# Modulated activations: who writes the rounded half of a high/low pair, and from where

## The chip, the cores and the metric

One core of a Trainium2 chip runs the whole program. The metric is device microseconds from launch to end, median of several executions; lower is better. Engine names in the profile: PE is TensorE, DVE is VectorE, ACT is ScalarE, POOL is GpSimd, SP is SyncE (it only issues transfers here).

## What is computed

Two small transformer blocks, one after the other, on 256 tokens of width 1024, all in float32. The change is in the second block, in the step that prepares the input of a matrix product: a norm, then a scale and a shift per feature (`modulate`). It occurs once for the pooled context, once for the context before the attention, and three times for the tokens.

```python
def rms_norm(x, g):
    y = x * lax.rsqrt(jnp.mean(x * x, axis=-1, keepdims=True) + EPS)
    return y * g

def modulate(h, shift, scale):
    return h * (1 + scale[:, None, :]) + shift[:, None, :]

# second_block, one layer
m_l = modulate(rms_norm(h_lat, norm_g[i, 1]), sh2, sc2)
h_lat = h_lat + g2[:, None, :] * sq_relu_mlp(m_l, mlp_w1[i], mlp_w2[i])
```

## The kernel before

Every product is made to float32 accuracy from three products of rounded halves: a matrix X is kept as a pair, X high (rounded to the type `F32R`) and X low (X minus its high half, in the same type), and `mm3` (lines 248 to 251) adds high x high, high x low and low x high in PSUM. Weights arrive by DMA as raw tiles of 128x1024; `split` makes their pair, with one activation on ScalarE (line 241) and two subtractions of 512 columns on VectorE (line 244), into a ring of seven slots. These "weight splits" run ahead of the products for the whole program.

An activation has 256 tokens, as two halves t of 128, and 1024 features, as 8 chunks k of 128 columns in the transposed layout. `mod_feed` (line 1102) handles one half t after the other, and in it four chunks at a time (n = 0, 1): VectorE scales the tokens by their reciprocal norm (line 1108, tile `mxn`), TensorE transposes four blocks into one PSUM bank of 512 columns (line 1111, tile `mtp`; two such banks take turns, and in the context's case they are shared with the products `cfo`), and then each block of 128 columns is multiplied by a column `g` and shifted by a column `b`, into the staging tile `m` (name `mmx`, two of them). `NACT` is 2: the first two of four blocks are done by ScalarE (line 1118), the others by VectorE (line 1120); in the call for layer 0 and the tokens all four are ScalarE's. Then `hilo_v` on VectorE makes the pair from `m`: a copy of 512 columns that rounds (line 259, a CAST in the profile), and a subtraction (line 260). With `mark` set, the last activation of half 0 becomes the mark `fed`: weight splits number 4 to 6 after it are told to wait for it on their engines.

`mod_xt` (line 1021) does the same for the pooled context, with 256 columns per chunk (both halves t) and two chunks per bank, so four banks; all scaling is ScalarE's (line 1038). Its staging tile shares a pool of three buffers with the two `mxn` tiles and others.

The order of the instructions on each engine is fixed when the program is built: a scheduler takes, for each engine, the ready instruction with the highest priority (by place in the program) by its own estimate of times. A buffer's next user waits until its last reader is done.

The places where these steps run, named here for later (start times in us of the profiled execution):

| place | what | lines | from, to |
|---|---|---|---|
| A | `mod_xt` in `ctx_pool`, beside the junction of `ple_block` | 1021 to 1040 | 1189, 1206 |
| B | `mod_feed` in `mlp0`, tokens, layer 0 | 1102 to 1124 | 1220, 1232 |
| C | `mod_feed` at the end of `mlp0`, context, layer 1; `cfo` products and `acc` products around it | 1102 to 1124, 1271 | 1552, 1574 |
| D | `mod_feed` in `attn_block` through `k_groups`, tokens; products `ckv` before, `lkv` behind | 1102 to 1124, 1348 | 1579, 1592 |
| E | `mod_feed` in `mlp1`, tokens, with `mark`; products `g` behind (24 per half) | 1102 to 1124, 1286 | 1708, 1730 |

Of the kernel before, what the change touches and what calls it, by code (L numbers as in the profile page):

```python
# [9 lines left out]
F32 = mybir.dt.float32  # L10
# [3 lines left out]
AF = mybir.ActivationFunctionType  # L14
ALU = mybir.AluOpType
# [8 lines left out]
NACT = 2  # L24
# [146 lines left out]
def tile_model(ctx: ExitStack, tc: tile.TileContext, A, out):  # L171
    nc = tc.nc
    V, S, G, T, Y = nc.vector, nc.scalar, nc.gpsimd, nc.tensor, nc.sync
# [24 lines left out]
    for t in range(2):  # L198
        for n in range(2):
            sl = slice(512 * n, 512 * n + 512)  # L200
# [57 lines left out]
    def hilo_v(hi, lo, src):  # L258
        V.tensor_copy(hi, src)
        V.tensor_tensor(lo, src, hi.bitcast(F32), op=ALU.subtract)  # L260

    def bank(r=None, name="bk"):
        r = r or M
        return r.bank.tile([128, 512], F32, name=name + r.tag, tag="bk" + r.tag)
# [22 lines left out]
    def rstd_of(src):  # L287
        return ms_r(ssq2(halves(src), 1.0 / 32), epst[:, 0:1])[1]
# [145 lines left out]
    def xk(xt, k, t):  # L434
        return xt[0][:, k, 128 * t:128 * t + 128], xt[1][:, k, 128 * t:128 * t + 128]
# [537 lines left out]
    gsc = cp.tile([128, 2, 2, 2, 8], F32, name="gsc")  # L973
# [47 lines left out]
    def mod_xt(src, l, v, j, sh, xt, al, r=None):  # L1021
        xn = []
        for t in range(2):
            rs = rstd_of(src[:, t])
            x = al([128, 1024], "mxn")
            V.tensor_scalar(x, src[:, t], rs, None, op0=ALU.mult)
            xn.append(x)
        for q in range(4):
            ps = bank(r, "mtp")
            for i in range(2):  # L1030
                for t in range(2):
                    T.transpose(ps[:, 256 * i + 128 * t:256 * i + 128 * t + 128],
                                xn[t][:, 256 * q + 128 * i:256 * q + 128 * i + 128], ident)
            m = al([128, 512], "mmx")
            for i in range(2):
                k = 2 * q + i
                sl = slice(256 * i, 256 * i + 256)
                S.activation(m[:, sl], ps[:, sl], AF.Identity, scale=gsc[:, l, v, j, k:k + 1], bias=sh[:, k:k + 1])
            hilo_v(xt[0][:, 2 * q:2 * q + 2].rearrange("p a c -> p (a c)"),
                 xt[1][:, 2 * q:2 * q + 2].rearrange("p a c -> p (a c)"), m)  # L1040

    def alloc_in(pool, bufs=2):
        def al(shape, name, dt=F32):
# [58 lines left out]
    def mod_feed(rr, l, v, j, sh, xt, al, src=None, r=None, mark=False):  # L1102
        src = h if src is None else src
        for t in range(2):
            rs = rr(t)
            for n in range(2):
                xn = al([128, 512], "mxn")
                V.tensor_scalar(xn, src[:, t, 512 * n:512 * n + 512], rs, None, op0=ALU.mult)
                ps = bank(r, "mtp")
                for i in range(4):  # L1110
                    T.transpose(ps[:, 128 * i:128 * i + 128], xn[:, 128 * i:128 * i + 128], ident)
                m = al([128, 512], "mmx")
                for i in range(4):
                    k = 4 * n + i
                    sl = slice(128 * i, 128 * i + 128)
                    g, b = gsc[:, l, v, j, k:k + 1], sh[:, k:k + 1]
                    if i < (4 if not l and not v else NACT):
                        sa = S.activation(m[:, sl], ps[:, sl], AF.Identity, scale=g, bias=b)
                    else:
                        V.tensor_scalar(m[:, sl], ps[:, sl], g, b, op0=ALU.mult, op1=ALU.add)  # L1120
                sl = (slice(None), slice(4 * n, 4 * n + 4), slice(128 * t, 128 * t + 128))
                hilo_v(xt[0][sl], xt[1][sl], m.rearrange("p (k c) -> p k c", k=4))
                if t == 0 and mark:
                    fed[:], cnt[:] = [sa.ins], [0]

# [7 lines left out]
    def ctx_pool(cx):  # L1133
        wk = cx.work
        al = u4(wk)
        hc = cx.sp.tile([128, 2, 1024], F32, name="hc", tag="hc")
        for t in range(2):
            Y.dma_start(hc[:, t], A["ctx"][128 * t:128 * t + 128])
        pool_pt(hc, hc, *prow(1, wk, "u4", 3), al, cx.xt, cx)
        hc = cx.sp.tile([128, 2, 1024], F32, name="hc", tag="hc")  # L1140
        for t in range(2):
            Y.dma_start(hc[:, t], A["ctx"][128 * t:128 * t + 128])
        gg = al([128, 1024], "crow")
        Y.dma_start(gg, rows[6].partition_broadcast(128))
        for n in range(2):
            w = split(cx, A["plw"], n)
            for t in range(2):
                ps = bank(cx, "cpm")
                for j in range(4):
                    g = 2 * n + j // 2  # L1150
                    sl = slice(256 * j, 256 * j + 256)
                    mm3(ps[:, 256 * (g % 2):256 * (g % 2) + 256], xk(cx.xt, 2 * g + j % 2, t), (w[0][:, sl], w[1][:, sl]),
                        j % 2 == 0, j % 2 == 1)
                y = al([128, 512], "cpy")
                V.tensor_tensor(y, ps, gg[:, 512 * n:512 * n + 512], op=ALU.mult)
                hs = hc[:, t, 512 * n:512 * n + 512]
                V.tensor_tensor(hs, hs, y, op=ALU.add)
        cx.hc = hc
        cx.xt = xt_tiles(8, cx.xp, "cxT")
        mod_xt(hc, 0, 1, 1, adacol[:, 0, 1, 24:32], cx.xt, al, cx)  # L1160
# [15 lines left out]
    def mlp0(rr, cx, pre):  # L1176
        with tc.tile_pool(name="lm0", bufs=1, reuse_waits="tile") as lm:
# [4 lines left out]
            xt = xt_tiles()  # L1182
            al = alloc_in(lm)
            mod_feed(rr, 0, 0, 1, adacol[:, 0, 0, 24:32], xt, al)

            def splits(w):
# [73 lines left out]
            def rstd(t):  # L1260
# [8 lines left out]
                return rstd_of(cx.hc[:, t])  # L1269

            mod_feed(rstd, 1, 1, 0, adacol[:, 1, 1, 0:8], cxt, al, cx.hc, cx)
            cx.xt = cxt
            for t in range(2):
# [7 lines left out]
    def mlp1(rr, cx):  # L1281
        with tc.tile_pool(name="lm1", bufs=1, reuse_waits="tile") as lm:
            g = gload(rows[8 + 3])
            xt = xt_tiles()
            al = alloc_in(lm)
            mod_feed(rr, 1, 0, 1, adacol[:, 1, 0, 24:32], xt, al, mark=True)

            def first():
# [345 lines left out]
```

## Time and profile before

| what | value |
|---|---|
| median of 3 executions | 1907.61 us (1907.52 to 1912.47) |
| the profiled execution | 1908.55 us |
| its span, first to last instruction | 1906.4 us |
| TensorE busy | 1838.0 us, 96% |
| VectorE busy | 1336.7 us, 70% |
| ScalarE busy | 923.3 us, 48% |
| GpSimd busy | 55.8 us, 3% |
| granted TensorE clock, mean | 0.991 of full speed |

Busy shares are means over the whole span; the stages of the change are five stretches of 10 to 22 us each, and a stage is read in the timeline of its own stretch: which engine stands still, and what ended its wait.

### The profile page before, as it was taken

The page shows a single profiled execution, that of the slowest core. Times are in us where ns is not written, and L with a number is a line of the kernel's source. Part 1 is how long each engine was busy: PE and PEld are TensorE (multiplying, and loading weights), DVE is VectorE, ACT ScalarE, POOL GpSimd, SP SyncE. Part 2 cuts the span into 40 slices and gives each one's busy share as a digit, 9 for nine tenths or more (in the row PEclk, how much of TensorE's full clock was granted, in tenths as well). Part 3 has the DMA queues.
Part 4 walks back from the last instruction along what each step waited for, and adds up shares of the span by engine and source line. Part 5 has one row for each costly group of instructions (what it writes and reads, how often), then busy time and mean ns, then how long its engine had stood idle before and what let it go on. Part 6 is the DMA issues. An engine that isn't in the chain of part 4 may idle for free.

```text
span 1906.4 us, 29714 instructions
## 1 busy us (share of the span) xinstructions
PE 1838.0 (96%) x11425; PEld 1617.3 (85%) x11425; DVE 1336.7 (70%) x2531; ACT 923.3 (48%) x1452; POOL 55.8 (3%) x96
## 2 busy tenths in 40 slices
PE   7999999999989999999999998899999999999998
PEld 6999777899969998888789897898999987667997
DVE  6997676899679986765587877854444468656555
ACT  6545656544474445444454455632322335544443
POOL 0000000000000000000000000000000002000000
PEclk9999999999999999999999999999999999999999
DMA  8887534788568876655488867433233224225662
GB/s 266 291 273 235 171 103 143 256 277 279 167 217 275 268 245 197 224 166 168 159 279 306 306 200 258 131 116 95 90 109 99 90 68 140 84 62 184 198 193 82
DMA packets 100950, 356.07 MB, mean 187 GB/s; under 512 B 12248, under 2 KB 13128, under 8 KB 100808
## 3 DMA queue, kind: packets, MB, share of 16 engines
q1 hardware_dynamic: 100088, 353.30, 57.0%
q8 instruction: 89, 1.46, 0.3%
q10 hardware_dynamic: 720, 0.88, 0.1%
q14 instruction: 53, 0.43, 0.1%
HBM read 353.03 MB, written 1.10 MB: 186 GB/s over the span
## 4 chain that ended last, share of the span: by engine, by line
PE 83%; DVE 6%; DMA 4%; ACT 3%; issue 2%; POOL 1%; SPq 0%; POOLq 0%; ACTq 0%; DVEq 0%
PE acc L249 8%; PE acc L251 8%; PE acc L250 8%; PE finm L249 7%; PE finm L250 7%; PE finm L251 7%; PE mfinm L249 3%; PE mfinm L251 3%; PE mfinm L250 3%; PE g L251 2%; PE g L249 2%; PE g L250 2%; DMA rawa<-in_adw_dram 2%; DVE wlm L244 2%; PE cfof L249 2%
## 5 line engine op out<-in xcount | busy, mean ns | idle before, releaser
L244 DVE TENSOR_TENSOR wlm<-rawm,whm 128x512 fp32r<-128x512 f32 x1048 | 683.5, 685 | 326.4 <-ACT whm L241 323.4
L241 ACT ACTIVATE whm<-rawm 128x1024 fp32r<-128x1024 f32 x524 | 548.3, 1057 | 506.2 <-PE acc L251 135.1
L249 PE MATMUL finm<-xTh,whm 128*128 128x256 f32 x1280 | 360.2, 281 | 1.3 <-DVE sil L495 1.3
L250 PE MATMUL finm<-xTl,whm 128*128 128x256 f32 x1280 | 359.7, 281 | 0.0
L251 PE MATMUL finm<-xTh,wlm 128*128 128x256 f32 x1280 | 359.6, 281 | 0.0
L251 PEld LDWEIGHTS finm<-xTh,wlm 128*128 128x128 f32 x1280 | 245.6, 192 | 0.0
L249 PEld LDWEIGHTS finm<-xTh,whm 128*128 128x128 f32 x1280 | 240.8, 188 | 4.1 <-DVE sil L495 2.3
L250 PEld LDWEIGHTS finm<-xTl,whm 128*128 128x128 f32 x1280 | 240.8, 188 | 1.4
L249 PE MATMUL acc<-whm,hidh 128*128 128x512 f32 x544 | 214.3, 395 | 3.1 <-ACT hidh L254 3.1
L251 PE MATMUL acc<-whm,hidl 128*128 128x512 f32 x544 | 214.2, 394 | 0.0
L250 PE MATMUL acc<-wlm,hidh 128*128 128x512 f32 x544 | 213.9, 394 | 0.0
L990 DVE SCALAR_TENSOR_TENSOR jka<-rawa,sv 128x1024 bf16<-128x1024 f32 x160 | 194.9, 1218 | 24.2 <-DMA rawa<-in_adw_dram 23.2
L249 PE MATMUL g<-whm,xTh 128*128 128x512 f32 x320 | 130.2, 407 | 10.4 <-ACT whm L241 3.8
L251 PE MATMUL g<-whm,xTl 128*128 128x512 f32 x320 | 131.0, 409 | 1.9 <-DVE xTl L346 1.2
L250 PE MATMUL mfinm<-xTl,whm 128*128 128x256 f32 x480 | 132.7, 277 | 0.0
L251 PE MATMUL mfinm<-xTh,wlm 128*128 128x256 f32 x480 | 132.7, 277 | 0.0
L249 PE MATMUL mfinm<-xTh,whm 128*128 128x256 f32 x480 | 132.7, 277 | 0.0
L250 PE MATMUL g<-wlm,xTh 128*128 128x512 f32 x320 | 128.4, 401 | 0.0
L249 PEld LDWEIGHTS acc<-whm,hidh 128*128 128x128 f32 x544 | 103.2, 190 | 24.4 <-ACT hidh L254 4.4
L250 PEld LDWEIGHTS acc<-wlm,hidh 128*128 128x128 f32 x544 | 103.0, 189 | 20.6 <-DVE wlm L244 0.2
L251 PEld LDWEIGHTS acc<-whm,hidl 128*128 128x128 f32 x544 | 102.7, 189 | 20.6
L250 PEld LDWEIGHTS mfinm<-xTl,whm 128*128 128x128 f32 x480 | 90.2, 188 | 0.6
(466 smaller groups left out, 3121.3 us busy)
## 6 DMA issues: line engine op xcount, KB each, us to landing
rawm<-in_m_dram SPq DMA_DIRECT2D x128, 512.0 KB, 4.0
rawa<-in_adw_dram SPq DMA_DIRECT2D x96, 512.0 KB, 5.3
rawm<-in_f1i_dram SPq DMA_DIRECT2D x88, 512.0 KB, 4.9
rawm<-in_f2i_dram SPq DMA_DIRECT2D x88, 512.0 KB, 4.8
rawm<-in_odi_dram SPq DMA_DIRECT2D x48, 512.0 KB, 4.5
rawm<-in_f1o_dram SPq DMA_DIRECT2D x40, 512.0 KB, 5.3
rawm<-in_f2o_dram SPq DMA_DIRECT2D x40, 512.0 KB, 4.9
rawm<-in_evi_dram SPq DMA_DIRECT2D x22, 512.0 KB, 4.3
```

Source lines behind the costliest of these rows:

```text
L241: a = S.activation(wh, src, AF.Copy)
L244: v = V.tensor_tensor(wl[:, sl], src[:, sl], wh[:, sl].bitcast(F32), op=ALU.subtract)
L249: T.matmul(o, a[0], b[0], start=first, stop=False)
L250: T.matmul(o, a[0], b[1], start=False, stop=False)
L251: T.matmul(o, a[1], b[0], start=False, stop=last)
L990: V.scalar_tensor_tensor(jk, src, 1.0, sv[v], op0=ALU.mult, op1=ALU.mult, accum_out=adacol[:, l, v, 2 * i + f:2 * i + f + 1])
```

## The change

The rounded high half is no longer copied from the staging tile. ScalarE computes scale and shift straight from PSUM and writes the rounded half, block by block, into its place. The unrounded value is computed a second time from the same bank into the staging tile, and VectorE subtracts the high half from it. In `mod_feed` the second computation is VectorE's for blocks 0 and 2 and ScalarE's for blocks 1 and 3, and the subtraction follows each pair of blocks (256 columns); the call for layer 0 no longer differs. In `mod_xt` all second computations are VectorE's, and the subtraction stays whole. The mark `fed` is the last of the new activations.

```diff
@@ mod_xt
             for i in range(2):
                 k = 2 * q + i
                 sl = slice(256 * i, 256 * i + 256)
-                S.activation(m[:, sl], ps[:, sl], AF.Identity, scale=gsc[:, l, v, j, k:k + 1], bias=sh[:, k:k + 1])
-            hilo_v(xt[0][:, 2 * q:2 * q + 2].rearrange("p a c -> p (a c)"),
-                 xt[1][:, 2 * q:2 * q + 2].rearrange("p a c -> p (a c)"), m)
+                g, b = gsc[:, l, v, j, k:k + 1], sh[:, k:k + 1]
+                S.activation(xt[0][:, k], ps[:, sl], AF.Identity, scale=g, bias=b)
+                V.tensor_scalar(m[:, sl], ps[:, sl], g, b, op0=ALU.mult, op1=ALU.add)
+            V.tensor_tensor(xt[1][:, 2 * q:2 * q + 2].rearrange("p a c -> p (a c)"), m,
+                            xt[0][:, 2 * q:2 * q + 2].rearrange("p a c -> p (a c)").bitcast(F32), op=ALU.subtract)
@@ mod_feed
                     g, b = gsc[:, l, v, j, k:k + 1], sh[:, k:k + 1]
-                    if i < (4 if not l and not v else NACT):
+                    sa = S.activation(xk(xt, k, t)[0], ps[:, sl], AF.Identity, scale=g, bias=b)
+                    if i % 2:
                         sa = S.activation(m[:, sl], ps[:, sl], AF.Identity, scale=g, bias=b)
+                        so = (slice(None), slice(k - 1, k + 1), slice(128 * t, 128 * t + 128))
+                        mv = m[:, 128 * i - 128:128 * i + 128].rearrange("p (k c) -> p k c", k=2)
+                        V.tensor_tensor(xt[1][so], mv, xt[0][so].bitcast(F32), op=ALU.subtract)
                     else:
                         V.tensor_scalar(m[:, sl], ps[:, sl], g, b, op0=ALU.mult, op1=ALU.add)
-                sl = (slice(None), slice(4 * n, 4 * n + 4), slice(128 * t, 128 * t + 128))
-                hilo_v(xt[0][sl], xt[1][sl], m.rearrange("p (k c) -> p k c", k=4))
                 if t == 0 and mark:
                     fed[:], cnt[:] = [sa.ins], [0]
```

## Rows read from the trace of the kernel before

A matmul or weight load has the line of `mm3` (249 to 251) or of its transpose; `DVE`, `ACT` and so on name the engine, and the names are those of the program's tiles.

**Rows 1.** The page, parts 1 and 4: busy time by engine; the chain.

```profile
PE 1838.0 (96%) x11425; PEld 1617.3 (85%) x11425; DVE 1336.7 (70%) x2531; ACT 923.3 (48%) x1452; POOL 55.8 (3%) x96
...
PE 83%; DVE 6%; DMA 4%; ACT 3%; issue 2%; POOL 1%; SPq 0%; POOLq 0%; ACTq 0%; DVEq 0%
```

**Rows 2.** Instructions of tile mmx: count, ns min/median/max, start times, shapes.

```profile
L1118 ACT ACTIVATE mmx<-mtpm,adacol,gsc x32: 447/458/503, 1221.6 to 1720.7; 128x128 f32<-128x128 f32 x32
...
L1120 DVE TENSOR_SCALAR mmx<-mtpm,gsc,adacol x16: 401/404/411, 1581.3 to 1721.9; 128x128 f32<-128x128 f32 x16
...
L259 DVE CAST xTh<-mmx x12: 414/418/420, 1223.7 to 1722.8; 128x512 fp32r<-128x512 f32 x12
...
L260 DVE TENSOR_TENSOR xTl<-mmx,xTh x12: 680/682/691, 1224.7 to 1723.8; 128x512 fp32r<-128x512 f32 x12
...
L1038 ACT ACTIVATE mmx<-mtpf,adacol,gsc x8: 556/563/570, 1189.3 to 1196.8; 128x256 f32<-128x256 f32 x8
```

**Rows 3.** Instructions by line and shape: busy us, mean ns, idle before.

```profile
L345 ACT ACTIVATE xTh<-tpsm,gct 128x128 fp32r<-128x128 f32 x96 | 31.3, 366 | 21.2 <-PE tpsm L337 16.3 <-DVE xTl L346 4.7
...
L255 DVE TENSOR_TENSOR hidl<-sil,hidh 128x256 fp32r<-128x256 f32 x80 | 33.4, 417 | 0.0
...
L244 DVE TENSOR_TENSOR wlm<-rawm,whm 128x512 fp32r<-128x512 f32 x1048 | 683.5, 685 | 326.4 <-ACT whm L241 323.4
```

**Rows 4.** Timeline of E, TensorE and ScalarE: start, us, instruction, idle before.

```profile
1711.86 0.51 PE L249 MATMUL g<-whm,xTh 128*128 128x512 f32 x1 [1.94 <-DVE xTh L259]
...
1719.70 1.50 ACT L1118 ACTIVATE mmx<-mtpm,adacol,gsc 128x128 f32<-128x128 f32 x4 [3.67 <-PE mtpm L1111]
...
1722.04 0.50 PE L249 MATMUL g<-whm,xTh 128*128 128x512 f32 x1 [1.47 <-DVE xTh L259]
...
1722.95 0.50 PE L251 MATMUL g<-whm,xTl 128*128 128x512 f32 x1 [0.19 <-DVE xTl L260]
```

**Rows 5.** Stretches: length; busy us of PE, PEld, DVE, ACT, POOL; PEclk; DMA.

```profile
1580.60:1582.20 1.60, 0.01 (x1) 0.02 (x1) 1.43 (x5) 1.60 (x7) 0.00 (x0) 1.00 0.91 248
...
1713.60:1717.00 3.40, 3.40 (x10) 2.63 (x9) 3.28 (x7) 2.42 (x4) 0.58 (x1) 0.51 0.50 157
...
1723.80:1727.20 3.40, 3.40 (x10) 2.62 (x9) 3.05 (x6) 1.32 (x2) 0.00 (x0) 0.50 0.60 180
...
1561.50:1567.20 5.70, 5.70 (x26) 4.69 (x25) 5.48 (x10) 4.00 (x7) 0.38 (x1) 1.00 0.06 6
...
1189.00:1199.40 10.40, 5.43 (x28) 4.47 (x27) 9.91 (x20) 8.65 (x18) 1.24 (x2) 0.78 0.39 106
```

**Rows 6.** Timeline of place A, VectorE and ScalarE.

```profile
1191.06 0.75 DVE L377 SCALAR_TENSOR_TENSOR h<-yt,rsm,h 128x512 f32<-128x512 f32 x1 [0.44 <-POOL rsm L308]
...
1200.13 1.42 DVE L377 SCALAR_TENSOR_TENSOR h<-yt,rsm,h 128x512 f32<-128x512 f32 x2 [0.77 <-POOL rsm L308]
...
1195.43 1.93 ACT L1038 ACTIVATE mmx<-mtpf,adacol,gsc 128x256 f32<-128x256 f32 x4 [0.29 <-PE mtpf L1032]
...
1197.24 0.64 ACT L301 ACTIVATE jkm<-pp 128x512 bf16<-128x512 f32 x1
```

**Rows 7.** Timeline of place B, ScalarE and TensorE.

```profile
1221.58 2.90 ACT L1118 ACTIVATE mmx<-mtpm,adacol,gsc 128x128 f32<-128x128 f32 x8 [0.44 <-PE mtpm L1111]
...
1227.51 0.50 PE L249 MATMUL cfof<-whm,hich 128*128 128x512 f32 x1 [1.08 <-ACT ac L1220]
```

**Rows 8.** Timeline of place C, VectorE and TensorE's weight loads.

```profile
1555.06 1.11 DVE L1120 TENSOR_SCALAR mmx<-mtpf,gsc,adacol 128x128 f32<-128x128 f32 x3 [1.20 <-ACT mmx L1118]
...
1555.90 0.19 PEld L249 LDWEIGHTS cfof<-whm,hich 128*128 128x128 f32 x1 [0.33 <-ACT mmx L1118]
```

**Rows 9.** Timeline of place D, ScalarE and TensorE.

```profile
1580.50 1.50 ACT L1118 ACTIVATE mmx<-mtpm,adacol,gsc 128x128 f32<-128x128 f32 x4
...
1582.21 0.63 PE L1111 MATMUL mtpm<-identt,mxn 128*128 128x128 f32 x4 [1.60 <-DVE mmx L1120]
...
1583.76 0.49 PE L251 MATMUL lkv<-whm,xTl 128*128 128x512 f32 x1
```

## The prediction

> **What bounds the kernel now.** I read the page first: TensorE is busy for 96% of the span and carries 83% of the chain that ended last; VectorE has 6% of the chain, ScalarE 3% [rows 1]. So an edit on VectorE or ScalarE counts only where TensorE waits for it. Second, the view of one tile, the staging tile of the modulated activations, finds every instruction that the change touches, in the five places A to E: 32 + 8 activations of 128 columns, 8 of 256, 16 + 8 VectorE scalings, 12 + 8 casts and as many subtractions (the second eight of each stand in the context's banks or tiles, in rows like those shown) [rows 2]. Third, the timeline of each place shows where TensorE stands still, and the stretches show the granted clock there [rows 4 to 9]. Outside these places nothing changes but the order that the scheduler writes.
>
> **What a bank costs.** A bank of four 128-column blocks is read now by two activations (start to start 0.347 us: four took 1.50 [rows 4]; one lasts 0.458 [rows 2]) and then by two VectorE scalings. VectorE does not begin with its half of the bank while ScalarE reads the other half: at C its first scaling starts at 1555.06, after 1.20 us of idleness, and what ended it was the activation, not the transposes [rows 8]. The other direction shows in the older feed step, where ScalarE stood 4.7 us in front of its next read of a bank, until VectorE had finished with the block before [rows 3]. I take it that all reads of one bank by two engines keep the program's order. Held time of a bank, before: 0.347 + 0.458 + 0.03 + 0.33 + 0.404 = 1.57 us. After, the order is ScalarE hi0; VectorE m0; ScalarE hi1, m1, hi2; VectorE m2; ScalarE hi3, m3: 0.458 + 0.404 + (2 x 0.347 + 0.458) + 0.404 + (0.347 + 0.458) + 4 hand-overs of 0.03 = 3.34 us, that is 1.77 longer (1.84 in B, where four activations of 1.50 made up the old chain). The other side of the ledger: the rounded half needs no cast of the whole bank any more. The first block's hi is there 0.46 us after the start, and its lo after hi0, m0, hi1, m1 and one subtraction of 256 columns (0.417 [rows 3]): 1.73 + 0.03 + 0.41 = 2.17 us, where the old chain needed 3.2 [rows 4].
>
> The rule of the Trainium skill, "PSUM — Partial Sum Buffer", section "PSUM bank collisions raise a hardware error", speaks against the change: reads of one bank by two engines must be kept apart, even on disjoint columns. If it didn't hold here, ScalarE alone would set the chain, 5 x 0.347 + 0.458 = 2.19 us in place of 3.34; that is the third rival below, and the rows side with the rule.
>
> **Engine work.** Each call of mod_feed issues per token half 12 activations in place of 4 (8 in B) and on VectorE 4 scalings and 4 subtractions of 256 columns in place of 4 scalings (none in B), 2 casts and 2 subtractions of 512. ScalarE: +8 x 0.347 = 2.8 us per half (B: +4, 1.4). VectorE: 4 x 0.404 + 4 x 0.417 = 3.28 against 4 x 0.404 + 2 x 0.418 + 2 x 0.682 = 3.82, so -0.5; in B against 2.20, so +1.1. In A ScalarE keeps 8 activations, and VectorE gets 8 scalings of 256 columns for 4 casts. No row shows that scaling: at least 0.405 (128 columns [rows 2]), at most 0.685 (512 columns, two inputs [rows 3]); with 1.04 ns per column, from 0.417 and 0.682 at 256 and 512, it is 0.404 + 0.133 = 0.54. VectorE in A: 8 x 0.54 - 4 x 0.418 = +2.6. That an activation writes the rounded type costs nothing: the one that does so now lasts 0.366 against 0.458 [rows 2, 3]. The Trainium skill, "ScalarE: Activation LUTs", section "What ACT_TABLE_LOAD costs", prices an activation with two pointer operands at 186 + 2 x 93 + 107 = 465 ns with 93 overlapped, an estimate of 372 ns each; eight would be 3.0 us, not 2.8. The row has 347, and I use that.
>
> **E, mlp1 (1708 to 1730): the gain.** TensorE stands for 1.94 us in the first half, for 1.47 and 0.19 in the second [rows 4]. Second half, from ScalarE's start T = 1719.70: the first product with a lo starts at 1722.95, T + 3.25; after, at T + 2.2. The two banks then share ScalarE, which puts lo23 at T + 3.9, and the products reach it at T + 3.6: 0.35 given back, net -0.7. The first half has the same chain, with two VectorE steps of the residual in front of its scalings in both versions: -0.7. Each pause is followed by 3.4 us at a granted clock of 0.50 to 0.51, which is 1.2 of 2.4 GHz, and these cost 1.7 us each; a pause of 1.60 us at D was followed by none (the lo product behind it lasts 0.49 us [rows 9], as the one in E does ahead of the drop, 0.50 [rows 4]). With the pauses cut by about a half I count on one of the two going: -1.7. Against it: the last activation of a half is the mark behind which three weight splits wait; it ends at about T + 5.1, not T + 1.5, and the split behind it feeds the products of chunks 6 and 7: +0.4. E: -2.7, from +0.5 (clock unchanged, marks late) to -4.8 (-1.4 - 3.4).
>
> **D, attn_block (1580 to 1592).** TensorE waits 1.60 us until bank 0 is read out, transposes the next half and only then starts the products, since these weren't ready earlier; the first lo product starts at 1583.76 [rows 9]. After, first hi at 1580.50 + 0.46 and first lo product at 1582.7: -1.0, less 0.35 for lo23: -0.7. The late bank (3.45 us) moves the next transposes to 1584, which the 24 products of the first half cover. From -1.5 to +1.0 (transposes left in front of the products).
>
> **C, end of mlp0 (1552 to 1574).** The products cfof wait for the bank, 0.33 us now [rows 8]; +1.77 later. Cover: 5.7 us in which TensorE, without a pause, does acc products that wait for nothing in C (the stretch from 1561.5 to 1567.2 [rows 5]). If the scheduler puts eight of them forward, nothing is lost; otherwise 1.77. I take +0.2.
>
> **B, mlp0 (1220 to 1232).** The second half's transposes need the first half's banks, 1.84 later each; ScalarE, which read eight blocks in one go [rows 7], is what TensorE waited for (1.08 us before cfof at 1227.51 [rows 7]), and gets 2.8 us more, VectorE 2.2. Prefetch splits can yield. I take +1.2, between 0 and +2.8.
>
> **A, mod_xt (1189 to 1206).** VectorE is busy for 9.91 of 10.40 us [rows 5] and owes the residual chain that leads to B; +2.6 less the 0.44 and 0.77 us that it idled for GpSimd [rows 6] leaves +1.4. It can come out at -1.8, since the sum of squares at 1197.24 stood behind four activations of 1.93 us [rows 6] that can now run before the staging tile is free, or at +2.6.
>
> **Sum:** 1.4 + 1.2 + 0.2 - 0.7 - 2.7 = -0.6 us. The profiled execution took 1908.55 us, 2.15 more than its span of 1906.4 and 0.9 above the median of 1907.61; so it would take 1907.9, and the median 1907.0.
>
> **Rivals.** (1) Faster, the clock: both stretches at half clock in E go (-4.8), D comes to its end (-1.5), and A's sum of squares gets ahead (-1.8), B and C 0: -8.1, 1899.5. For it: the pause of 1.60 us at D without a drop. Against: the drop after 1.47. (2) Slower, the hand-overs: each bank now goes from ScalarE to VectorE and back twice, and VectorE's queue is full of weight splits of 0.685 us [rows 3] that stand in front. The path meets some eight banks (two in A, B and E, one in C and D); with a wait of w per hand-over to VectorE it loses 16 w. The change is slower than before from w = 0.04 us, and by 0.3% (5.7 us) from w = 0.39; with one split each time, w = 0.6, it is +9.0, 1916.6. For it: the places A and B, where VectorE is never idle. Against: in E it has little else to do, and the scheduler places the urgent step first. (3) The reads of a bank aren't kept apart: 1.15 us less per bank, eight banks, -0.6 - 9.2: 1897.8. Rows 3 and 8 speak against it.
>
> **How the numbers follow.** About 0.3% is what a measurement of this kernel can tell from no change. The forecast 0.72, rival 1 0.11, rival 2 0.14, rival 3 0.03. The forecast's own range is 1903 to 1911 (the ends of E and A one way or the other, not all together); to leave out no more than 2 in 10 it is stretched toward both rivals, 1901.5 to 1913.5. Faster 0.14, same 0.73, slower 0.13.
>
> **What would show it.** In the profile after: 64 activations that write hi and 32 that write the staging tile in mod_feed, no casts from the staging tile; VectorE's scalings each after an activation of the same bank; banks held 3.3 us; in E the third product 2.2 us after ScalarE's start and one stretch at half clock; in A and B TensorE idle longer by 1 to 2 us. I'm wrong if the order of work outside A to E moves the time, if a bank is held under 2.5 or over 4.5 us, or if E's clock stays as it is.

## The result

The changed kernel is slower: 1918.69 us median of 7 executions (1914.61 to 1923.11) against 1907.61 of 7 of the kernel before; ratio 1.0051, interval 1.0038 to 1.0064. A second set of it (e10 below) gave 1.0045, 1.0029 to 1.0061. The forecast was 1907.0, within 0.3% of no change. The profiled execution took 1915.77 us, with a span of 1914.0: 7.6 us more than the span of before.

### The profile page after: what moved, and what is told of

Its sections match the earlier page's. It is cut to its first block, busy times and chain, and to the rows that moved or that the text cites. A ratio compares the mean times of both kernels' runs of the same rounds, so it can differ in the third digit from the quotient of the medians.

```text
span 1914.0 us, 29806 instructions
## 1 busy us (share of the span) xinstructions
PE 1838.6 (96%) x11425; PEld 1617.0 (84%) x11425; DVE 1338.5 (70%) x2543; ACT 942.3 (49%) x1508; POOL 55.7 (3%) x96
## 4 chain that ended last, share of the span: by engine, by line
PE 79%; DVE 7%; DMA 6%; ACT 4%; issue 2%; POOL 1%; SPq 0%; POOLq 0%; ACTq 0%; DVEq 0%
PE acc L249 8%; PE acc L251 8%; PE acc L250 8%; PE finm L249 7%; PE finm L251 7%; PE finm L250 7%; DMA rawa<-in_adw_dram 3%; PE mfinm L249 3%; PE mfinm L251 3%; PE mfinm L250 3%; PE g L251 2%; PE g L249 2%; PE g L250 2%; DVE wlm L244 2%; PE cfinf L249 1%
## 5 line engine op out<-in xcount | busy, mean ns | idle before, releaser
L249 PEld LDWEIGHTS mfinm<-xTh,whm 128*128 128x128 f32 x480 | 90.1, 188 | 2.5 <-ACT mmx L1121 1.9
```

Source lines behind the costliest of these rows:

```text
L249: T.matmul(o, a[0], b[0], start=first, stop=False)
```

## The profile after

The page of the kernel after, parts 1 and 4 (against [rows 1]):

```profile
PE 1838.6 (96%) x11425; PEld 1617.0 (84%) x11425; DVE 1338.5 (70%) x2543; ACT 942.3 (49%) x1508; POOL 55.7 (3%) x96
...
PE 79%; DVE 7%; DMA 6%; ACT 4%; issue 2%; POOL 1%; SPq 0%; POOLq 0%; ACTq 0%; DVEq 0%
```

TensorE's work is the same; ScalarE has 56 activations and 19 us more; on the chain, TensorE gave up four points: two went to DMA, one each to VectorE and ScalarE. The tile `mmx` after (against [rows 2]; line 1119 holds the activations that write hi, 1121 and 1126 the staging tile, 1124 the subtractions of mod_feed, 1040 the scalings of mod_xt):

```profile
L1126 DVE TENSOR_SCALAR mmx<-mtpm,gsc,adacol x24: 397/406/414, 1225.0 to 1731.2; 128x128 f32<-128x128 f32 x24
L1121 ACT ACTIVATE mmx<-mtpm,adacol,gsc x24: 447/482/614, 1225.8 to 1732.8; 128x128 f32<-128x128 f32 x24
L1124 DVE TENSOR_TENSOR xTl<-mmx,xTh x24: 411/424/426, 1226.5 to 1733.9; 128x256 fp32r<-128x256 f32 x24
L1040 DVE TENSOR_SCALAR mmx<-mtpf,gsc,adacol x8: 534/536/544, 1191.7 to 1201.4; 128x256 f32<-128x256 f32 x8
```

The single prices were right: no cast is left, a subtraction of 256 columns takes 424 ns (417 assumed), a scaling of 256 columns 536 (540 estimated). What is different is who waits. Place A on TensorE (timeline: start, us, instruction, idle before and what ended it):

```profile
1194.06 1.08 PE L1032 MATMUL mtpf<-identt,mxn 128*128 128x128 f32 x4 [4.28 <-DVE mmx L1040]
1198.10 1.09 PE L1032 MATMUL mtpf<-identt,mxn 128*128 128x128 f32 x4 [2.96 <-DVE mmx L1040]
1201.63 0.55 PE L249 MATMUL cfinf<-cxTh,whm 128*128 128x256 f32 x1 [2.44 <-DVE mmx L1040]
```

Before, the same three waits were 0.55, 3.53 and 0.90 us, and ScalarE ended them:

```profile
1190.39 0.66 PE L1032 MATMUL mtpf<-identt,mxn 128*128 128x128 f32 x4 [0.55 <-ACT mmx L1038]
1194.58 1.02 PE L1032 MATMUL mtpf<-identt,mxn 128*128 128x128 f32 x4 [3.53 <-ACT mmx L1038]
...
1196.50 0.58 PE L249 MATMUL cfinf<-cxTh,whm 128*128 128x256 f32 x1 [0.90 <-ACT mmx L1038]
```

Now each bank comes free with VectorE's second scaling, which lies in VectorE's order among the residual's steps and the weight splits. Stretches of A, of B and of E (columns as in [rows 5]), then B on ScalarE and TensorE:

```profile
1194.00:1198.00 4.00, 1.08 (x4) 0.71 (x4) 4.00 (x9) 3.88 (x9) 0.94 (x2) 0.50 0.04 16
...
1226.00:1230.00 4.00, 2.74 (x15) 1.87 (x14) 3.93 (x10) 4.00 (x12) 0.00 (x0) 1.00 0.55 180
1230.00:1234.00 4.00, 2.65 (x13) 1.66 (x11) 3.98 (x13) 4.00 (x12) 0.00 (x0) 1.00 0.26 96
...
1716.00:1737.00 21.00, 16.82 (x79) 12.83 (x77) 17.23 (x38) 17.16 (x39) 1.12 (x2) 1.00 0.31 97
```

```profile
1225.48 0.46 ACT L1119 ACTIVATE xTh<-mtpm,adacol,gsc 128x128 fp32r<-128x128 f32 x1 [0.37 <-DVE mmx L1126]
...
1228.44 0.66 PE L1113 MATMUL mtpm<-identt,mxn 128*128 128x128 f32 x4 [1.26 <-ACT mmx L1121]
...
1234.13 0.38 PE L249 MATMUL mfinm<-xTh,whm 128*128 128x256 f32 x1 [1.49 <-ACT mmx L1121]
```

In A VectorE has no free moment, in B ScalarE has none and VectorE hardly any. The activation at 1225.48 stood 0.37 us until VectorE had done its block of the same bank: the rule of the Trainium skill ("PSUM — Partial Sum Buffer", section "PSUM bank collisions raise a hardware error") that two engines' reads of one bank are kept apart agrees with this row. Place D on VectorE and on TensorE (against [rows 9]):

```profile
1589.35 0.35 DVE L1371 SCALAR_TENSOR_TENSOR ckn<-ckv,rsf,ckgb 128x128 f32<-128x128 f32 x1 [1.13 <-POOL rsf L284]
1589.62 0.41 DVE L1124 TENSOR_TENSOR xTl<-mmx,xTh 128x256 fp32r<-128x256 f32 x1
```

```profile
1587.14 0.51 PE L249 MATMUL lkv<-whm,xTh 128*128 128x512 f32 x1 [0.39 <-ACT xTh L1119]
1587.49 0.39 PE L250 MATMUL lkv<-wlm,xTh 128*128 128x512 f32 x1
1589.76 0.33 PE L1374 MATMUL cktpf<-identt,ckn 128*128 128x128 f32 x1 [1.88 <-DVE ckn L1371]
1590.09 0.50 PE L251 MATMUL lkv<-whm,xTl 128*128 128x512 f32 x1
```

The first product now starts early, as forecast, but the first lo stands in VectorE's order behind `ckn`, a step of the context's keys that waits 1.13 us for GpSimd, and the first lo product in TensorE's order behind the transpose `cktpf` of that `ckn`. In the kernel before, VectorE did the first lo ahead of `ckn`:

```profile
1583.02 0.68 DVE L260 TENSOR_TENSOR xTl<-mmx,xTh 128x512 fp32r<-128x512 f32 x1
...
1585.67 0.35 DVE L1367 SCALAR_TENSOR_TENSOR ckn<-ckv,rsf,ckgb 128x128 f32<-128x128 f32 x1 [0.27 <-POOL rsf L284]
```

In E (against [rows 4]) the waits have changed their place, and little of their sum: 1.76 + 1.47 = 3.23 us against 1.94 + 1.47 + 0.19 = 3.60. First TensorE, then ScalarE in the first half:

```profile
1722.79 0.50 PE L251 MATMUL g<-whm,xTl 128*128 128x512 f32 x1 [1.76 <-DVE xTl L1124]
...
1725.91 0.63 PE L1113 MATMUL mtpm<-identt,mxn 128*128 128x128 f32 x4 [1.47 <-DVE mxn L1110]
```

```profile
1719.79 0.90 ACT L1119 ACTIVATE xTh<-mtpm,adacol,gsc 128x128 fp32r<-128x128 f32 x2 [2.37 <-PE mtpm L1113]
1720.86 0.63 ACT L1101 ACTIVATE jkm<-h 128x512 bf16<-128x512 f32 x1 [0.18 <-DVE h L1099]
...
1721.49 0.44 ACT L1119 ACTIVATE xTh<-mtpm,adacol,gsc 128x128 fp32r<-128x128 f32 x1
```

The first lo product starts 3.0 us after ScalarE's first hi, not 2.2 as forecast: between the first hi of the two banks and the next one, ScalarE's order has `jkm`, a sum of squares of the residual.

The next table is the account of all traces, in us between first starts that the timelines show: A from its first transpose to the first of B; B to the first `rl` of mlp0; C from its first `hc` to the first transpose of D; D to the first square of `lkv`; "attention" to the last `lkv` product of line 249; E to the first `rl` of mlp1; "behind E" to the last `accf` product of line 249. In brackets: how many stretches of 3.4 us at half clock (1.2 of 2.4 GHz) lie in it. From B's end to C it is 310.7 to 311.2 in all. The time ahead of A varies by 9 us between traces of the same instructions (1182.1 to 1191.3), so places are compared, not spans.

| trace | A | B | C | D | attention | E | behind E |
|---|---|---|---|---|---|---|---|
| before | 35.8 (2) | 16.2 | 31.7 | 17.0 | 54.1 | 79.2 (2) | 166.7 |
| after | 38.5 (4) | 18.7 | 32.7 | 19.7 (1) | 55.6 (1) | 75.4 | 167.5 |
| e10 after again | 38.9 (4) | 18.6 | 32.7 | 19.6 (1) | 54.0 | 75.5 (1) | 171.5 (1) |
| e1 A only | 38.1 (3) | 17.6 | 32.0 | 17.0 | 54.1 | 79.1 (2) | 166.5 |
| e2 B only | 35.9 (2) | 21.6 (3) | 31.7 | 17.1 | 54.0 | 76.6 | 167.1 |
| e3 D only | 35.8 (2) | 16.2 | 31.7 | 19.7 (1) | 54.0 | 76.8 | 168.9 (1) |
| e4 E only | 35.8 (2) | 16.2 | 31.7 | 17.0 | 54.1 | 77.7 (2) | 166.7 |
| e5 | 37.0 (2) | 20.2 (2) | 32.3 | 18.4 (1) | 57.7 (1) | 77.7 (1) | 166.8 |
| e6 | 37.7 (3) | 17.7 (1) | 31.8 | 17.0 | 54.1 | 76.6 | 167.4 |
| e7 | 35.8 (2) | 21.6 (2) | 31.7 | 17.0 | 54.1 | 79.2 (2) | 166.7 |
| e8 | 35.8 (2) | 16.2 | 31.7 | 17.2 | 55.4 | 78.9 (2) | 167.0 |
| e9 | 35.6 (2) | 16.2 | 31.7 | 15.8 | 57.3 | 79.2 (2) | 166.4 |
| e11 | 35.6 (2) | 16.2 | 31.8 | 15.8 | 57.3 | 77.3 (2) | 166.7 |
| e12 | 35.8 (2) | 16.3 | 31.7 | 18.4 | 55.6 (1) | 79.2 (2) | 166.4 |
| e13 | 37.8 (1) | 18.6 | 32.7 | 18.4 | 54.0 | 75.6 | 171.2 (1) |
| e14 | 35.6 | 16.2 | 31.7 | 17.0 | 54.2 | 76.7 | 168.5 (1) |

## The experiments

The first theory: each place pays or gains by itself. A, B and D pay, because a bank goes from ScalarE to VectorE and back and because the new steps stand behind others in an engine's order; E gains. The rivals stand with each run.

**One place at a time (e1 to e4).** The new form in one place, the old one elsewhere; for e3, with `mod_feed2` the new form:

```diff
-        kps, cxt = k_groups(cx, xt, lambda: mod_feed(rr, 1, 0, 0, ...))
+        kps, cxt = k_groups(cx, xt, lambda: mod_feed2(rr, 1, 0, 0, ...))
```

> Only mod_xt (place A) has the new form, mod_feed is as before. Theory (each place pays or gains by itself, as the two traces' times along the span say): B begins 2.6 us later than before, nothing gives it back, the end comes 2.6 us later, ratio 1.0014. Rival (the delay of a place is taken up by slack further on, or arises only together with the others): under 0.8 us at the end, ratio 1.0004 or less.

Measured 1.0019 (1.0006 to 1.0032). A is 2.3 us longer, and B, in the old form, 1.4 more: what A delays runs on into B.

> Only the feed step of mlp0 (place B) has the new form. Theory: ScalarE is busy without a break from 1226 to 1234, the products mfinm begin 2.5 us later, the end comes 2.5 us later, ratio 1.0013. Rival (ScalarE was full there only because A delivered late): under 0.8 us, 1.0004 or less.

Measured 1.0011 (0.9996 to 1.0026). B is 5.4 us longer, not 2.5, with three stretches at half clock that B does not have when A is changed too. In these traces A and B don't add: 2.3 + 1.4 + 5.4 = 9.1 alone, 5.35 together. But the traced execution of e2 has one of the two lowest mean clocks of its twelve, 0.988 against up to 0.993, and the medians of e2 and of the kernel before are only 2.8 us apart: the 5.4 us belong to this execution, three stretches included, more than to the form. By the ratios, 1.0019 and 1.0011, A and B cost 3.6 and 2.1 us alone, each to within some 2.5 us, and that does add up to about what they cost together. TensorE in e2, and a stretch of it:

```profile
1228.86 1.97 PE L1135 MATMUL mtpm<-identt,mxn 128*128 128x128 f32 x8 [2.64 <-ACT mmx L1143]
...
1229.80:1231.80 2.00, 2.00 (x8) 1.81 (x8) 1.70 (x5) 1.39 (x4) 0.00 (x0) 0.50 0.03 8
```

> Only the feed step of attn_block (place D) has the new form. Theory: the lo subtraction again stands behind ckn and GpSimd in VectorE's order, first lo product 2.5 us later relative to D's start, and 2.7 to 4.2 us at the end of attention and at the end, ratio 1.0014 to 1.0022. Rival (D is late in the changed kernel because of what the earlier places did to the weight splits): within 0.8 us of the kernel before at the end of attention.

Measured 1.0015 (1.0002 to 1.0028). D is 2.7 us longer, as in the changed kernel, with the same wait of 1.88 us for `ckn`; the earlier places have nothing to do with it.

> Only the feed step of mlp1 (place E) has the new form. Theory: both stretches at half clock go away and E ends 4.0 us earlier than before; behind E the changed kernel lost 1.3 us again, so 2.7 to 4.0 us at the end, ratio 0.9979 to 0.9986: faster than both kernels. Rival (E's gain in the changed kernel is only slack that the late attention had made, such as weight splits that were already done when E began): under 1 us, ratio 0.9995 or more.

Measured 1.0010 (0.9992 to 1.0027): no gain. Both stretches at half clock are there in the new form (two), while the old form has none in e2, e3 and e6. That the clock held in E in the first trace of the changed kernel was not the change's doing. The traced execution, 1903.72 us, is the fastest of the twelve (median 1910.04), so it doesn't show what the others lose.

**Who reads the bank, and in which order (e5 to e8).** In e5 the instructions of each engine are the change's, but ScalarE reads a bank first and VectorE afterwards (here `mod_feed`; `mod_xt` likewise):

```diff
+                for i in range(4):
+                    S.activation(xk(xt, kk[i], t)[0], ps[:, cs[i]], AF.Identity, ...)
+                for i in (1, 3):
+                    S.activation(m[:, cs[i]], ps[:, cs[i]], AF.Identity, ...)
+                for i in (0, 2):
+                    V.tensor_scalar(m[:, cs[i]], ps[:, cs[i]], ...)
```

> The changed kernel with the same instructions on each engine, only in another order per bank: ScalarE does all its reads of a bank, then VectorE does its own (mod_xt: hi0, hi1, then m0, m1; mod_feed: hi0 to hi3, m1, m3, then m0, m2). One hand-over from ScalarE to VectorE per bank where the change has two, and none back. Theory (the hand-overs, each behind other work in VectorE's queue, make the loss): about half of it goes, first cfinf 13 to 14.5 us after the first transpose of A (16.6 in the changed kernel, 11.4 before), D 1 to 2 us longer than before instead of 3.8, ratio 1.0025. Rival (the added work on VectorE in A and on ScalarE in B, whatever its order): 1.0045 to 1.0055 again, cfinf at 16 to 17 us.

TensorE in A of e5:

```profile
1192.22 0.63 PE L1032 MATMUL mtpf<-identt,mxn 128*128 128x128 f32 x4 [3.02 <-DVE mmx L1044]
1194.99 1.09 PE L1032 MATMUL mtpf<-identt,mxn 128*128 128x128 f32 x4 [2.14 <-DVE mmx L1044]
1197.12 0.55 PE L249 MATMUL cfinf<-cxTh,whm 128*128 128x256 f32 x1 [1.04 <-DVE mmx L1044]
```

The waits are 6.20 us in place of 9.68, `cfinf` starts 12.7 us after A's first transpose in place of 16.6, and A is 1.2 us longer than before, not 2.9 (the mean of the two traces of the changed kernel). So with the same work, the order of the reads made more than half of A's loss, as far as A goes. But B lost 4.0 us with two stretches at half clock, and A and B together take 57.2 us in e5 and 57.2 and 57.5 in the changed kernel, with four stretches at half clock in each: what the order gave in A was gone at B's end. Attention lost 3.6, and the whole measured 1.0054 (1.0040 to 1.0069). The theory holds for A and not for the sum.

e6: ScalarE alone reads the bank in A (two activations for each block, VectorE only subtracts).

> Only mod_xt (A) changed: ScalarE writes hi and m, both from PSUM, VectorE only subtracts. VectorE reads no bank here and loses the casts too. Theory (VectorE's queue in front of its reads of the bank made A's loss): the first cfinf 11.4 to 12.5 us after the first transpose of A, B's rl no later than before, ratio 0.9995 to 1.0005. Rival (a bank that is read twice as often is late whoever reads it; ScalarE gets 4.5 us more): cfinf at 13.5 us or more, ratio 1.001 to 1.002.

Measured 1.0011 (0.9999 to 1.0023); `cfinf` at 12.6 us, A 1.9 and B 1.5 us longer: 3.4 together, against 3.7 in e1, where VectorE makes the second reading. `cfinf` comes 4.0 us earlier than in e1 (16.6), and by the end of B that has gained 0.3. So nearly all of what A costs is there without any hand-over to VectorE, with the second reading of each bank on ScalarE.

e7: in B ScalarE writes the four hi (four activations per bank, as before), VectorE the four blocks of `m`.

> Only the feed step of mlp0 (B) changed: ScalarE writes the four hi of a bank and nothing else (four activations, as before), then VectorE the four blocks of m. Theory (in B it is ScalarE, busy without a break, that delays; one hand-over per bank is cheap): from the first transpose of B to the first rl of mlp0 16.2 to 17.0 us without clock loss (16.2 before, 18.7 in the changed kernel, 21.6 in e2 of which 5.1 to the clock); ratio 1.0000 to 1.0005. Rival (VectorE's hand-over and its added 1.2 us per bank): 18 us or more, 1.001 or more.

Measured 1.0020 (1.0008 to 1.0032), B 5.4 us longer in a trace with two stretches at half clock, the lowest mean clock of its twelve executions (0.986 against up to 0.991); the medians are 3.7 us apart. The theory of a full ScalarE falls: relieving it brings nothing. TensorE in B of e7 now waits for VectorE, which has no free moment there (second fence):

```profile
1227.60 0.66 PE L1135 MATMUL mtpm<-identt,mxn 128*128 128x128 f32 x4 [1.79 <-DVE mmx L1143]
1229.54 0.66 PE L1135 MATMUL mtpm<-identt,mxn 128*128 128x128 f32 x4 [1.29 <-DVE mmx L1143]
1231.58 0.55 PE L249 MATMUL mfinm<-xTh,whm 128*128 128x256 f32 x1 [1.38 <-DVE mmx L1143]
```

```profile
1226.00:1230.00 4.00, 1.11 (x8) 0.84 (x8) 4.00 (x13) 2.95 (x8) 0.00 (x0) 1.00 0.23 91
1230.00:1234.00 4.00, 2.62 (x13) 2.45 (x12) 4.00 (x14) 1.50 (x4) 0.00 (x0) 0.54 0.02 4
```

In the changed kernel both engines are full in B, in e7 VectorE is; the second read of the bank costs whichever of them gets it.

e8: the banks are read as before, and in C, D and E only the cast moves to ScalarE, from the staging tile, in halves.

> A version of my own: the banks are read as in the kernel before (m0, m1 ScalarE, m2, m3 VectorE: the bank is held as short as before) in C, D and E; the cast goes to ScalarE, from the staging tile, in halves of 256 columns, and the subtraction follows in halves. A and B as before. Theory (the bank's hold is the cost, an early first half the gain): E from the last lkv to the first rl 1.3 us or more shorter than before at the same clock (77.8 with and 74.5 with no half-clock stretch), D not longer than before, ratio 0.9985 to 0.9995. Rival (E's gain came from hi straight from PSUM, and more work on ScalarE costs by itself): E as before within 0.5 us, ratio 1.0000 or more.

Measured 1.0027 (1.0016 to 1.0037). E is 0.3 us shorter at the same two stretches, not 1.3, and attention 1.3 longer. The rival stands: E's shorter time comes from hi straight from PSUM, and added work on ScalarE costs by itself.

**D: the neighbour in the order (e9, e11), and the changed kernel again (e10).** e9 is e3 with one line: the first half's `ckn` may be issued only behind the fourth lo.

```diff
-                V.scalar_tensor_tensor(kn[:, sl], pc[:, t, sl], ...)
+                with after(los[3] if t == 0 else None):
+                    V.scalar_tensor_tensor(kn[:, sl], pc[:, t, sl], ...)
```

> Only the feed step of attn_block (D) has the new form, as in e3, and the first token half's ckn may not be issued before the fourth lo subtraction: what stood in front of the lo in VectorE's order now stands behind it. Theory (the queue neighbour that waits for GpSimd made D's loss): the first lo product starts 2.4 to 2.7 us after ScalarE's first hi (3.4 in e3, 3.3 before), from the first ckv product to the first square of lkv 29.0 to 30.0 us with no stretch at half clock (29.4 before, 32.0 in e3 of which 1.7 to the clock), ratio 0.9995 to 1.0005. Rival (the bank held twice as long and ScalarE's added reads make it): 31 us or more, a stretch at half clock again, ratio 1.001 to 1.002.

TensorE in e9, at the first lo product and later:

```profile
1584.24 0.50 PE L251 MATMUL lkv<-whm,xTl 128*128 128x512 f32 x1 [1.29 <-DVE xTl L1148]
...
1597.63 1.10 PE L1400 MATMUL cktpf<-identt,ckn 128*128 128x128 f32 x4 [1.06 <-DVE ckn L1397]
```

The first lo product starts 2.5 us after ScalarE's first hi (3.4 in e3, 3.3 before). D is 15.8 us: 1.2 shorter than before, where e3 is 2.7 longer, and no stretch at half clock is left. So in D it was the neighbour: of the 3.9 us between e3 and e9 nothing is due to the bank, which both read alike. But `ckn` is now late for the second half (TensorE waits 1.06 us for it, 0.82 before), and attention takes 57.3 us in place of 54.1. D and attention together take 73.1 us in e9, 73.6 in e3 and 71.1 before: putting `ckn` back gives 0.5 of the 2.5 us, and the whole measured 1.0015 (1.0002 to 1.0028), as e3 did.

> The changed kernel once more, for a second trace and more times. Theory (in the first trace and in the single-place runs the clock loses 1.7 us per stretch, in A, in D and behind it because TensorE waits there, in E now and then in either form): stretches at half clock again add 1.7 to 3.5 us in A or B and 1.7 in D over the kernel before, E anything from 0 to 3.4; time lost to the clock over all executions 4 to 5 us more than before, the rest 4 to 5 us more too; ratio 1.0045 to 1.0055. Rival (the stretches of the first trace came by chance): no added stretch in A, B and D, loss to the clock as before within 1 us.

Measured 1.0045. A, B, C and D repeat the first trace within 0.4 us; in E and behind it the clock falls once each.

> e9 and the new form in E, A to C as before: the version that could beat both kernels. Theory: E 1.3 us shorter than before at the same loss to the clock, D not longer: ratio 0.9988 to 0.9998. Rival (what E's early products gain is given back behind E, where products run ahead of their weight splits): 0.9998 to 1.0010.

Measured 1.0020 (1.0008 to 1.0031). E is 1.9 us shorter than in e9 at the same two stretches, and the whole no faster.

**The clock (e12 to e14).** By (1 - mean granted clock) x span, the clock cost 17.6 us in the mean of 87 executions of the kernel before, and 22.5 and 23.6 in the two sets of the changed kernel: 5 to 6 of the 9 us that it is slower, by that count. To see whether TensorE's waiting brings the stretches, and what they cost, it gets products whose result nobody reads while it waits; all else keeps its order. e12, on e3:

```diff
+        tps0 = bank(cx, "cktp")
+        for _ in range(6):
+            T.matmul(tps0, xk(xt, 0, 0)[0], ws[0][0][:, 0:512], start=True, stop=True)
```

> e3 (only D new) with six extra products of 512 columns on TensorE, whose result is overwritten unread, right behind the first transposes of D and ahead of the first lkv product: 1.4 us of work in a place where TensorE waits 1.88 us for ckn; all other instructions stand in the order of e3. Theory (the waiting of TensorE is what brings the stretch at half clock in D, which came in four traces of four with the new form and in none of the others): no stretch at half clock there, from the first ckv product to the first square of lkv 30.2 to 30.8 us (32.0 in e3, of which 1.7 to the clock; 29.4 before). Rival (the stretch comes from something else, such as the load of all engines there): the stretch stays, 32.0 to 32.5 us.

e12 on TensorE, and the stretch behind the wait in e12 and (second fence) in e3:

```profile
1578.46 1.65 PE L1387 MATMUL cktpf<-whm,xTh 128*128 128x512 f32 x6 [0.39 <-ACT xTh L1141]
...
1581.07 0.33 PE L1399 MATMUL cktpf<-identt,ckn 128*128 128x128 f32 x1 [0.50 <-DVE ckn L1396]
...
1581.00:1584.40 3.40, 3.33 (x18) 2.60 (x18) 2.95 (x10) 2.15 (x7) 0.00 (x0) 1.00 0.03 8
```

```profile
1586.90:1590.30 3.40, 3.40 (x11) 2.58 (x12) 2.46 (x8) 1.16 (x3) 0.00 (x0) 0.54 0.00 0
```

The clock stays up, 18 matmuls in 3.4 us in place of 11, and D is 18.4 us in place of 19.7. So in D the half clock does follow the wait, and costs 1.3 of the 2.7 us. In e12 attention takes them back, 55.6 us with a stretch of its own at half clock against 54.0 in e3; in e13, with the same products in D, it does not (54.0). The whole of e12 measured 1.0007 (0.9997 to 1.0016), and the interval of e3, 1.0015, overlaps it.

e13 does the same in A (20 products in its three waits) and D of the changed kernel, e14 in A (10 products) and E (14 repeated transposes) of the kernel before.

> The changed kernel with extra products on TensorE whose result nobody reads, in the places where it waits: in A 5 before the transposes of the third bank, 12 before those of the fourth and 3 before the first cfinf (512 columns each, into a bank of their own), in D the six of e12. All other instructions of every engine in the order of the changed kernel. Theory (half of the change's loss is clock, and the clock falls because TensorE waits): the loss to the clock over all executions goes back to 17 to 20 us (22.5 and 23.6 in the two sets of the changed kernel, 17.6 in the kernel before), the rest stays 4 to 5 us above before, ratio 1.0020 to 1.0030. Rival (the clock falls for another reason in A): loss to the clock 21 us or more, ratio 1.0035 to 1.005.

> The kernel before with such extra work: in A ten products of 512 columns between the transposes of the third and the fourth bank, where TensorE waits 3.53 us, and in E eight and six repeated transposes behind those of each half, where it waits 1.94 and 1.47 us. All other instructions in the order of before. Theory: the loss to the clock falls by 1.7 to 5 us (A lost 3.4 in each trace of the old form, E 3.4 in about half), ratio 0.9975 to 0.9990: faster than both kernels. Rival (the clock falls in A and E for another reason): 0.9997 to 1.0005.

The first 36 us from A's start, in the changed kernel and in e13, then in the kernel before and in e14:

```profile
1185.00:1221.00 36.00, 26.04 (x181) 23.96 (x182) 33.63 (x65) 20.71 (x39) 5.96 (x7) 0.81 0.36 116
```

```profile
1190.70:1226.70 36.00, 30.64 (x207) 27.26 (x208) 34.05 (x67) 21.40 (x41) 5.73 (x7) 0.95 0.36 116
```

```profile
1185.10:1221.10 36.00, 30.62 (x210) 27.83 (x211) 33.36 (x67) 22.92 (x45) 5.11 (x8) 0.91 0.40 126
```

```profile
1183.90:1219.90 36.00, 31.37 (x222) 27.55 (x223) 33.43 (x67) 22.92 (x45) 5.37 (x8) 1.00 0.39 126
```

The clock came back (0.81 to 0.95, 0.91 to 1.00), and the time did not. e13 measured 1.0059 (1.0043 to 1.0075) though its executions lost only 18.2 us to the clock, 2.6 more than the 15.6 of the kernel before in the same series; e14 measured 1.0006 (0.9996 to 1.0016) with 12.6. In A of e14 no half clock is left and B starts 0.2 us earlier: VectorE is busy for 33.4 of 36 us in either, so the half clock of TensorE lay beside it. In E of e14 2.5 us are gained, and 1.8 are lost again behind it, where a stretch at half clock has come. The extra products have a price of their own: in A of e13 they hold up the transposes behind them, and `cfinf` starts 17.0 us after A's first transpose, not 16.6. My second theory, that half of the loss is the clock's, falls; of A's loss at most 0.7 to 1.1 us goes with it (37.8 against 38.5 and 38.9).

No version beat the kernel before: e14 and e12 came nearest.

## Why the prediction was wrong

The account by places, the mean of the two traces of the changed kernel against the kernel before: A +2.9, B +2.45, C +1.0, D +2.65, attention +0.7 (+1.5 and -0.1). E with what lies behind it: 245.25 us in the mean of the eight traces with the old form there (before, e1 to e3, e6, e7, e9, e12), 245.0 in the five with the new one (after, e4, e10, e11, e13): -0.2. Together +9.5, measured +9.1 (means of 7 and 6 against 87 executions). The forecast had -0.6, and these steps of it failed:

**D, -0.7, measured +2.65: the largest miss, and of sign.** In D the chain of the bank was right (e9: -1.2, the first lo product 2.5 us after ScalarE's first hi, 2.2 forecast). I worked it out as if VectorE and TensorE had nothing else to do. In the kernel before, `ckn` stood behind the first lo in VectorE's order; in the new one the scheduler puts it ahead, and it waits for GpSimd. This was not in the range (+1.0 at most). Half of it is the half clock that follows the wait of 1.88 us (e12); I had written that D's pause of 1.60 us brings no drop, which is true of the kernel before. The attention behind D had no term in the sum. It needs one: with `ckn` put back, D and attention together still take 2.0 us more than before (e9), and why is not shown.

**E, -2.7, measured -0.2: the term of the clock.** The drops come and go in either form (old: two, two, none, none, none, two, two, two; new: none, two, one, two, none), so the "-1.7" was a reading of one trace. The rest of the step, -1.4 + 0.4 = -1.0, stands at equal clock: with two stretches in E and none behind, E and what lies behind it take 244.4 and 244.0 us in the new form (e4, e11) against 245.6 to 245.9 in the old (before, e1, e7, e9, e12); with none, 242.9 (after) against 243.7 and 244.0 (e2, e6). The path was not the one forecast, since the first lo product came at 3.0 us and not at 2.2. What spoils the mean are e10 and e13, 171.5 and 171.2 us behind E. They have a stretch at half clock there, as e3 and e14 have (168.9 and 168.5), and then their products of 256 columns follow each other more slowly, with no wait and at a granted clock of 1.00: the starts lie 118 ns apart in the mean, 113 to 115 in the other traces. Line 251 of `mfinm` behind E, ns min/median/max of one, in the first trace of the changed kernel and in e10:

```profile
L251 PE MATMUL mfinm<-xTh,wlm x218: 276/276/282, 1744.8 to 1887.9; 128*128 128x256 f32 x109
...
L251 PE MATMUL mfinm<-xTh,wlm x215: 276/281/282, 1744.9 to 1889.6; 128*128 128x256 f32 x108
```

4 ns on each of some 650 such products are 2.6 us, an estimate that matches the 2.6 and 2.7 us by which e10 and e13 exceed e3 and e14. The same kernel has it in one trace and not in the other, so it is not a cost that the form brings each time. The whole times show no gain from E's form either: e4 measured 1.0010 (0.9992 to 1.0027), e11 1.0020 against e9's 1.0015.

**A, +1.4, measured +2.9 (upper end +2.6).** Of the two waits for GpSimd that I subtracted as cover [rows 6], the 0.77 us gave way and the 0.44 is still there. Within A the added work is only part of it: e5, with the same work and one hand-over per bank, has +1.2, so the order of the reads makes 1.7. By the end of B that difference is gone (e5, e6).

**B, +1.2, measured +2.45 (upper end +2.8).** Inside its range. That ScalarE is what TensorE waits for was right, but relieving ScalarE brings nothing (e7). A and B together have +5.35 against +2.6 forecast. That is what their two upper ends give, 2.6 + 2.8, so by the sum the idle time and the yielding splits that I counted as cover were worth nothing.

**C, +0.2, measured +1.0.** The scheduler put the acc products in front of the late bank, as forecast; half of the price appears later, where the products `ckv` wait for the context's lo:

```profile
1579.94 0.50 PE L251 MATMUL ckv<-whm,cxTl 128*128 128x512 f32 x1 [0.19 <-DVE cxTl L1124]
...
1581.93 0.50 PE L251 MATMUL ckv<-whm,cxTl 128*128 128x512 f32 x1 [0.33 <-DVE cxTl L1124]
```

**The rivals.** The second one, hand-overs behind VectorE's queue, +9.0 with a chance of 0.14, has the sign and nearly the sum, but that is luck: the order of the reads costs 1.7 us within A (e5) and next to nothing by the end of B (e5, e6), and D comes from an order that it didn't have. The third is out: the reads of a bank are kept apart. Of the signs that I named, the casts' disappearance, the order of the reads and TensorE's longer idleness in A and B came; a bank was held 3.5 us in E (1719.79 to 1723.33) against 3.3 forecast; the third product of E at 2.2 us did not come (3.0), nor, in the first trace, the one stretch at half clock. My sentence on being wrong "if the order of work outside A to E moves the time" was the nearest to what happened, though it was the order inside D.

**A sum that is wrong.** In the working 186 + 2 x 93 + 107 is 479, not 465, and less 93 it is 386, not 372 (eight: 3.1 us, not 3.0). No term of the forecast was worked out from it.

**What stays open.** Why the products behind E are slower in two traces; why D and attention together lose 2 us with `ckn` in either place; what of B's loss in e2 and e7 would be left in a trace without stretches at half clock; and when E's clock falls.

## What to carry to other kernels

A shorter chain through one tile gains nothing until you have asked where its steps will stand in each engine's order: look at the neighbour that the scheduler could put in front of them, and at what that neighbour waits for. A second reading of a bank is work for an engine: where both that could do it are full, neither who does it nor in which order makes it free. In A, letting each engine do all its reads of a bank at once shortened TensorE's waits from 9.68 to 6.20 us, and no whole time was better for it. Follow a gain or a loss to the end of the next stage before you book it: D's gain in e9 was gone in attention, A's in e5 was gone in B. And don't count a half-clock stretch as time lost, nor its absence as gained, from one trace: see first whether TensorE was what the stretch waited for, and whether the drop is there in other traces of the same form.

## What was not expected of the hardware

In D the granted clock fell to half behind a wait of 1.87 or 1.88 us (after, e10, e3, e5), and stayed up behind 1.60 (before, [rows 9]), behind 0.39 and 1.29 (e9) and with the wait filled but for 0.39 and 0.50 (e12). In attention it fell behind a wait of 1.88 us (after) and of 1.90 (e12), and stayed up behind 1.88 or 1.89 (e3, e10, e13) and behind 2.21 and 2.22 (e9, e11). In E it stayed up behind 1.76 and 1.47 us in the changed kernel, and fell behind the same two in e4; it fell behind 1.94 and 1.47 in the kernel before ([rows 4]) but not in e2, e3 and e6, which have the same instructions there and the same two waits (1.94 and 1.48). So the same instructions meet the drop in one execution and not in the next, and a wait of a given length doesn't decide it by itself.
